# A two-layer decoder step on one Trainium2 core: two small results go through DRAM instead of TensorE, and the sample's low parts take 128 columns

## The chip, the cores and the metric

The kernel runs on one core of one Trainium2 chip. A core has five engines with their own instruction queues: TensorE (PE, matrix products; PEld is its loading of the stationary operand), VectorE (DVE), ScalarE (ACT), GpSimd (POOL) and SyncE (SP, which here issues nearly all DMA transfers). Each engine works through its own queue in the order in which it was written and meets the others through semaphores only. The metric is the device time of one execution in microseconds (us). Smaller is better.

## The reference

One inference step of a decoder trunk with two layers, model width 1024, for 256 prompt tokens and 64 sample tokens (8 sequences of 8) with shared weights. All arrays are float32. Layer 0 mixes tokens with a spatial-gating MLP, layer 1 with a matrix memory (mLSTM); after each comes a gated MLP with a short convolution; each sub-layer has an RMSNorm ahead of it.

```python
def rmsnorm(x, g):
    y = x32 * lax.rsqrt(jnp.mean(x32 * x32, axis=-1, keepdims=True) + EPS)
    return y * g
def chunk_spatial_gating(x, w_in, ln_g, ln_b, w_s, b_s, w_out):       # layer 0
    h = jax.nn.gelu(x @ w_in);  u, v = jnp.split(h, 2, axis=-1)
    v = (v32 - mu) * lax.rsqrt(var + EPS) * ln_g + ln_b               # mean, variance over a row of v
    ws = jnp.where(mask, w_s[:, :L, :L], 0.0)                         # lower triangle, 8 groups of 128 x 128
    mixed = jnp.einsum('gts,bnsgd->bntgd', ws, vc) + b_s
    return (u * mixed) @ w_out, v
def mlstm_mixer(x, ...):                                              # layer 1
    p = x @ w_in            # q, k (then a convolution of width 4), v, an output gate, two small gates
    ...                     # chunkwise matrix memory, norm over heads
    return (o * hn) @ w_out, ...
def trunk(x, ...):
    for i in range(2):
        x = x + mixer_i(rmsnorm(x, norm_mix_g[i]))
        x = x + conv_ffn(rmsnorm(x, norm_ffn_g[i]), ...)
    return rmsnorm(x, final_norm_g), ...
```

Because the mixing over tokens is linear, the kernel applies `ln_b` behind it: the mixed bias is `ln_b` times the sum of a row of the masked mixing matrix `ws`. These row sums (8 groups x 128 rows) are one of the two small results that the change moves.

## The kernel before

**Precision.** Every large product is made from two halves. A float32 value is split into a high part, rounded to the type float32r in which TensorE is fed, and a low part, the rest: `wh` and `wl` for weights (`prefetch`: ScalarE writes `wh`, L180, VectorE subtracts for `wl`, L181), `xh` and `xl` for activations. A product is then `wh*xh + wh*xl + wl*xh`, three matmuls.

**Weights.** They come from DRAM in blocks of 128 x 1024 (`raw`, four buffers, issued on SP's queue), and are split into `wh` and `wl` (three buffers) up to two blocks ahead of the matmuls that use them. A `raw` buffer is free for the next transfer when `wl` has been written.

**Two forms of product.** Most stages hold the weights stationary and stream 320 tokens (`rows`, tile `pm`). For the values of both mixers the tokens are stationary and 512 weight columns stream (tiles `pv` for two groups of 128 prompt tokens and `pvs` for the sample). There are only 64 sample tokens, so the sample's stationary operand `xs` holds 128 columns, its high parts and its low parts. One matmul with `wh` then gives both `xh*wh` and `xl*wh` in different rows of the result, and the rows are added afterwards. A second matmul adds `xh*wl`.

- Layer 0 (`columns`, `first_rows`): `xs` is 64 high columns and then 64 low ones; the matmul with `wl` takes the 64 high columns alone, `pv[2][:64]`. There are four passes `q` over 512 columns of v, each of eight steps `k`; a step is two times three matmuls for the prompt and two for the sample. The final product (`own`, t = 2) does the same with 256 streamed columns.
- Layer 1 (`values`): high and low columns alternate in groups of 16. `xs` has 256 columns per step: 128 with high and low parts for `wh`, 128 with high parts and zeros for `wl`.

**Norms.** The weights of a norm are folded into `xh` and `xl`; the factor per token is applied to a product's result. `norm_cols` (L258) gives the factors as columns `rc` (one per token, tokens on partitions): a sum of squares by three small matmuls against ones (`pc`), VectorE (`ms`) and a power on GpSimd. `norm_row` (L284) makes from them the row `rb`, the factors of all 320 tokens on every partition: it splits `rc`, puts the halves on diagonals (`dg`) and multiplies by ones on TensorE (`pb`). Layer 0 calls `norm_cols` in pass q = 1 and `norm_row` behind pass q = 2; `rb` is first read when block 0 of u is done (L540). Layer 1 has `norm_twice` (L271) as well, which makes one more column of factors `rc2` for the sample in the doubled layout of `xs`.

**Row sums.** `load_ws` fetches the mixing matrix behind pass q = 1 and GpSimd masks it. `row_sums`, behind pass q = 2, splits it (in a pair of the weights' buffers) and multiplies it by ones, four matmuls into `pr`; ScalarE copies the sums, the same on every partition, to `rsum` (`rs_a`, L407). VectorE uses them for `b2` (L522, named `b` in the trace), the bias of a block of mixed values. The first two `b2` stand in VectorE's queue between the splits of weight blocks.

**Order.** TensorE's instructions are pinned to the order in which the program writes them. The queues of the other engines are put in order ahead of time by a scheduler with its own estimate of durations, so a changed dependence can also move other rows. Once built, each queue is fixed: an instruction that waits holds up all that stand behind it.

Of the kernel before, what the change touches and what calls it, by code (L numbers as in the profile page):

```python
# [39 lines left out]
class Net:  # L40
# [215 lines left out]
    def norm_cols(self, parts=None):  # L256

        nc = self.nc  # L258
        parts = parts or [self.acc]
# [11 lines left out]
    def norm_twice(self):  # L271

        nc = self.nc
        acc2 = self.tp.tile([P, P], F32, tag="acc2", name="acc2", bufs=1)
        nc.scalar.copy(self.spread(acc2), self.twice(self.acc[:, TP:]))
        pc = self.psa.tile([P, 512], F32, tag="pa", name="pc2")
        self.mm(pc[:, 0:2], acc2, self.ones[:, :2], True, True)
        ms = self.tp.tile([P, 1], F32, tag="ms2", name="ms2", bufs=1)
        rc = self.tp.tile([P, 1], F32, tag="rc2", name="rc2", bufs=1)
        nc.vector.tensor_scalar(ms, pc[:, 0:1], 1.0 / D, EPS, op0=MULT, op1=ADD)  # L280
        nc.gpsimd.tensor_tensor(rc, ms, self.mhalf, op=ALU.pow)
        self.rc2 = rc

    def norm_row(self):  # L284
# [6 lines left out]
        for half in range(2):  # L291
# [3 lines left out]
            nc.vector.tensor_scalar(dg[:, half, TP:], self.ident[:, 64:], rc[:, half, 2:3], None, op0=MULT)  # L295
# [52 lines left out]
    def residual_norm(self, m, ps, gcol):  # L348
# [3 lines left out]
        if gcol == V_MIX + 8:  # L352
            rows = self.xs[:, m, :].rearrange("p (j g d s) -> p j d g s", j=2, g=4, d=2)
            xh, xl = [x[:, m, TP:].rearrange("p (g s) -> p g s", g=4) for x in (self.xh, self.xl)]
            self.nc.gpsimd.tensor_copy(rows[:, :, 0], xh.unsqueeze(1).to_broadcast([P, 2, 4, 16]))
            self.nc.gpsimd.tensor_copy(rows[:, 0, 1], xl)
# [14 lines left out]
    def layer_a(self):  # L371
        nc, tc, I, O = self.nc, self.tc, self.I, self.O
        with tc.tile_pool(name="ya", bufs=1) as yp, tc.tile_pool(name="la", bufs=1) as lp:
# [8 lines left out]
            rsum = lp.tile([P, NH, P], F32, name="rs_a")  # L382
            trit = lp.tile([P, P], F32, name="trit")
            bdt = lp.tile([P, 64], F32, name="bdt")

            def load_ws():
                nc.sync.dma_start(ws, I["a_ws"])
                nc.sync.dma_start(trit, I["trit"])
# [23 lines left out]
            def first_rows(k, pv, wh, wl):  # L412
# [3 lines left out]
                for i in range(2):  # L416
# [8 lines left out]
                    self.mm(pv[2][:64, c], xs[:, :64], wl[:, c], False, False)  # L425

            def columns(q, k, pv, wh, wl):
# [28 lines left out]
            for q in range(4):  # L456
# [22 lines left out]
                if q == 2:  # L479
                    self.norm_row()  # L480
                    row_sums()
# [151 lines left out]
    def final(self, block, yh, yl, lp):  # L633
# [59 lines left out]
        def own(k, t):  # L693
# [14 lines left out]
            else:  # L708
                xs = yh[:, k, TP:TP + P]
                self.mm(a[:64], xs[:, :64], wl, False, False)  # L710
                self.mm(a, xs, wh, False, last)
# [37 lines left out]
    def layer_b(self):  # L749
# [5 lines left out]
        with ExitStack() as ctx:  # L755
# [8 lines left out]
            mxb = lp.tile([P, 64], F32, name="mxb")  # L764
            gm = lp.tile([P, 4, NH], F32, name="gm")
# [722 lines left out]
```

## Time and profile before

| | before |
|---|---|
| device time, median of 3 runs (lowest to highest) | 942.83 us (942.75 to 943.12) |
| span of the profiled execution, first to last instruction | 941.1 us |
| what lies around the span, taken against the median | 1.7 us |
| TensorE busy | 934.1 us (99%) |
| VectorE, ScalarE, GpSimd busy | 684.5, 508.4, 105.0 us |
| mean granted TensorE clock | 0.998 of full speed |
| DMA moved | 156.46 MB, mean 166 GB/s |

The profile gives no separate time for the profiled execution beside its span; the 1.7 us is the median less the span. Times of day in the trace (such as 49.96) are microseconds from the start of the span. Three things help in reading it. A matmul's recorded duration contains the time its results need to drain, and the next one starts before that is over: what a matmul costs in a row of them is the distance from its start to the next start. `pvs<-wl,xh 128*64 128x512` is a matmul that writes `pvs` from the streamed `wl` (512 columns) with a stationary `xh` of 128 partitions by 64 columns. And the summary of waits names, for an engine and a line, what it waited for, in all, how often, and the longest.

### The profile page before, as it was taken

How to read it: one execution, taken by the hardware profiler on the slowest of the kernel's cores; microseconds unless marked ns; L12 is line 12 of the kernel's file. 1: busy time of each engine (PE TensorE's matmuls, PEld its weight loads, DVE VectorE, ACT ScalarE, POOL GpSimd, SP SyncE). 2: the span in 40 equal slices, each digit the busy share in tenths (PEclk: the TensorE clock that was granted, in tenths of full speed). 3: DMA queues.
4: the chain of work that ended last, by engine and by line, in shares of the span. 5: the costliest groups of instructions: out<-in, count | busy, mean ns of one | idle time of the engine just before them, and what ended most of it. 6: DMA issues, size and time to landing. Idle time of an engine off the chain costs nothing.

```text
span 941.1 us, 16815 instructions
## 1 busy us (share of the span) xinstructions
PE 934.1 (99%) x6361; PEld 902.4 (96%) x6361; DVE 684.5 (73%) x1258; ACT 508.4 (54%) x893; POOL 105.0 (11%) x316
## 2 busy tenths in 40 slices
PE   9999999999999999999999999999999999999997
PEld 8789999999999999998989989989999999999997
DVE  6668975587777765458998988787689777775541
ACT  7567544445544543346777776475656545544332
POOL 3200000011000001113221201000002111100001
PEclk9999999999999999999999999999999999999999
DMA  8746444544555554457675747645474555545621
GB/s 289 223 131 178 133 131 148 155 143 150 156 151 144 154 152 144 146 169 221 210 244 170 232 165 230 228 134 168 151 214 154 144 151 155 146 144 153 202 82 56
DMA packets 58272, 156.46 MB, mean 166 GB/s; under 512 B 6912, under 2 KB 19976, under 8 KB 58192
## 3 DMA queue, kind: packets, MB, share of 16 engines
q1 hardware_dynamic: 58048, 155.13, 53.7%
q8 instruction: 50, 0.82, 0.4%
q10 hardware_dynamic: 144, 0.26, 0.1%
q14 instruction: 30, 0.25, 0.1%
HBM read 143.42 MB, written 11.95 MB: 165 GB/s over the span
## 4 chain that ended last, share of the span: by engine, by line
PE 97%; DVE 1%; POOL 0%; issue 0%; ACT 0%; POOLq 0%; DVEq 0%; ACTq 0%
PE pm L49 76%; PE pv L49 9%; PE pvs L49 3%; PE num L49 2%; PE pyt L49 1%; PE pmix L49 1%; PE py L49 1%; PE pCp L49 1%; PE pcs L49 1%; PE psc L49 0%; PE pw L49 0%; PE phn L52 0%; DVE bcv L903 0%; DVE wl L181 0%; PE pk L52 0%
## 5 line engine op out<-in xcount | busy, mean ns | idle before, releaser
L180 ACT CAST wh<-raw 128x1024 fp32r<-128x1024 f32 (+4 forms) x252 | 255.0, 1013 | 289.4 <-PE pm L49 159.8
L181 DVE TENSOR_TENSOR wl<-raw,wh 128x1024 fp32r<-128x1024 f32 (+4 forms) x252 | 297.0, 1180 | 118.2 <-ACT wh L180 117.2
L49 PE MATMUL pm<-xh,wh 128*128 128x320 f32 x1088 | 338.5, 311 | 0.0
L49 PE MATMUL pm<-xh,wl 128*128 128x320 f32 x1088 | 336.2, 309 | 0.0
L49 PE MATMUL pm<-xl,wh 128*128 128x320 f32 x1088 | 336.1, 309 | 0.0
L49 PEld LDWEIGHTS pm<-xh,wh 128*128 128x128 f32 x1088 | 204.3, 188 | 1.7 <-ACT wh L180 0.5
L49 PEld LDWEIGHTS pm<-xl,wh 128*128 128x128 f32 x1088 | 204.4, 188 | 0.2
L49 PEld LDWEIGHTS pm<-xh,wl 128*128 128x128 f32 x1088 | 204.2, 188 | 0.0
L49 PE MATMUL pm<-yh_f,wh 128*128 128x320 f32 x308 | 95.2, 309 | 0.0
L49 PE MATMUL pm<-yl_f,wh 128*128 128x320 f32 x308 | 94.9, 308 | 0.0
L49 PE MATMUL pm<-yh_f,wl 128*128 128x320 f32 x308 | 94.9, 308 | 0.0
L49 PEld LDWEIGHTS pm<-yl_f,wh 128*128 128x128 f32 x308 | 57.8, 188 | 0.0
L49 PEld LDWEIGHTS pm<-yh_f,wh 128*128 128x128 f32 x308 | 57.8, 188 | 0.0
L49 PEld LDWEIGHTS pm<-yh_f,wl 128*128 128x128 f32 x308 | 57.8, 188 | 0.0
L590 DVE SCALAR_TENSOR_TENSOR fcv<-fpad,vecs,fcv 128x336 f32<-128x336 f32 x88 | 49.7, 565 | 1.5
L49 PE MATMUL pv<-wh,xh 128*128 128x512 f32 (+1 forms) x132 | 50.6, 389 | 0.0
L49 PE MATMUL pv<-wh,xl 128*128 128x512 f32 (+1 forms) x132 | 50.3, 386 | 0.0
L49 PE MATMUL pv<-wl,xh 128*128 128x512 f32 (+1 forms) x132 | 50.1, 385 | 0.0
L346 DVE TENSOR_TENSOR xT<-pm,xT 128x320 f32<-128x320 f32 x38 | 18.6, 491 | 32.9 <-PE pm L49 32.9
L49 PE MATMUL pm<-yhb,wh 128*128 128x320 f32 x128 | 39.9, 312 | 0.0
L49 PE MATMUL pm<-yh_a,wh 128*128 128x320 f32 x128 | 39.6, 309 | 0.0
L49 PE MATMUL pm<-yl_a,wh 128*128 128x320 f32 x128 | 39.5, 309 | 0.0
(340 smaller groups left out, 1461.8 us busy)
## 6 DMA issues: line engine op xcount, KB each, us to landing
raw<-in_f_up SPq DMA_DIRECT2D x88, 512.0 KB, 3.6
raw<-in_b_win SPq DMA_DIRECT2D x32, 512.0 KB, 3.9
raw<-in_f_dn SPq DMA_DIRECT2D x28, 448.0 KB, 3.3
C<-in_C SPq DMA_DIRECT2D x32, 258.0 KB, 5.6
raw<-in_a_win SPq DMA_DIRECT2D x16, 512.0 KB, 3.6
raw<-in_a_wo SPq DMA_DIRECT2D x16, 512.0 KB, 3.7
raw<-in_b_wv SPq DMA_DIRECT2D x16, 512.0 KB, 3.4
out_Cs<-C SPq DMA_DIRECT2D x32, 256.0 KB, 4.6
```

Source lines behind the costliest of these rows:

```text
L49: self.pin(self.nc.tensor.matmul(out, lhsT, rhs, start=start, stop=stop))
L180: self.last_split = nc.scalar.copy(wh[:, c, :], raw[:, c, :])
L181: self.last_low = nc.vector.tensor_tensor(wl[:, c, :], raw[:, c, :], wh[:, c, :].bitcast(F32), op=SUB)
L346: self.nc.vector.tensor_tensor(x, ps[:, :T], x, op=ADD)
L590: nc.vector.scalar_tensor_tensor(cv, pd[:, i:i + NC], self.vec(w + i * KF), cv, op0=MULT, op1=ADD)
```

## The change

1. **Layer 0, norm row** (`norm_sent`): no `norm_row`. SP writes the factors `rc`, 256 prompt and 64 sample values, to a row of 320 numbers in DRAM by two transfers and reads this row back to all 128 partitions as `rb`.
2. **Layer 0, row sums**: the mixing matrix is loaded a second time in its natural layout (`wn`, 512 KB, rows on partitions). GpSimd masks it (`affine_select`), VectorE adds over a row (`tensor_reduce` into `rs8`, 128 x 8), SP writes these 1024 numbers to DRAM, transposed, and reads all of them back to every partition as `rsum`. No split of the matrix and no `pr`.
3. **Layer 1, norm**: the sample's sums of squares are doubled into the layout of `xs` first (`twofold`, a ScalarE copy that was there before inside `norm_twice`), and `norm_cols` takes them for its third column. `rc` then holds the doubled sample factors, `norm_twice` is gone, and `norm_row` takes every sample token once with a loaded 0/1 matrix `pick`.
4. **Sample's low parts**: the matmul with `wl` takes the same 128 columns as the one with `wh`, in layer 0, in layer 1 and in the final product. The term `xl*wl`, left out before, is now added. In layer 1 `xs` shrinks to 128 columns a step, without the zeros that GpSimd wrote at the start of the kernel and with less to copy. In layer 0 and the final product the matmul with `wh` now always comes first.

The core of the diff:

```diff
-    def norm_cols(self, parts=None):
+    def norm_cols(self, side=None):
...
         for t in range(3):
-            for i, a in enumerate(parts):
-                self.mm(pv[:, t, :], self.tokens(a, t), self.ones[:, :2], i == 0, i == len(parts) - 1)
+            a = side if side is not None and t == 2 else self.tokens(self.acc, t)
+            self.mm(pv[:, t, :], a, self.ones[:, :2], True, True)
...
-    def norm_twice(self):
+    def twofold(self):
         acc2 = self.tp.tile([P, P], F32, tag="acc2", name="acc2", bufs=1)
-        nc.scalar.copy(self.spread(acc2), self.twice(self.acc[:, TP:]))
-        pc = self.psa.tile([P, 512], F32, tag="pa", name="pc2")
-        self.mm(pc[:, 0:2], acc2, self.ones[:, :2], True, True)
...
+        self.nc.scalar.copy(self.spread(acc2), self.twice(self.acc[:, TP:]))
+        return acc2
+
+    def norm_sent(self):
+        nc, rows = self.nc, self.I["norm"]
+        nc.sync.dma_start(rows[:, :TP].rearrange("o (t p) -> p (o t)", p=P), self.rc[:, :2])
+        nc.sync.dma_start(rows[:, TP:].rearrange("o p -> p o"), self.rc[64:, 2:])
+        self.rb = self.tp.tile([P, T], F32, tag="rb", name="rb", bufs=1)
+        nc.sync.dma_start(self.rb, rows.to_broadcast([P, T]))
...
             def load_ws():
                 nc.sync.dma_start(ws, I["a_ws"])
+                nc.sync.dma_start(wn, I["a_wsn"])
...
             def row_sums():
-                wh = self.wsp.tile([P, 8, P], F32R, tag="wh", name="wh")
-                wl = self.wsp.tile([P, 8, P], F32R, tag="wl", name="wl")
-                self.split(wh, wl, ws)
-                one = self.ones.bitcast(F32R)
-                for i in range(2):
-                    pr = self.psa.tile([P, 512], F32, tag="pa", name="pr")
-                    for j, w in enumerate((wh, wl)):
-                        self.mm(pr, one, w[:, 4 * i:4 * i + 4, :], j == 0, j == 1)
-                    nc.scalar.copy(rsum[:, 4 * i:4 * i + 4, :].rearrange("p g t -> p (g t)"), pr)
+                nc.gpsimd.affine_select(wn, wn, pattern=[[0, NH], [-1, P]], compare_op=ALU.is_ge, fill=0.0, base=0, channel_multiplier=1)
+                nc.vector.tensor_reduce(rs8, wn, axis=mybir.AxisListType.X, op=ADD)
+                nc.sync.dma_start(I["rsum"].rearrange("g t -> t g"), rs8)
+                nc.sync.dma_start(rsum, I["rsum"].rearrange("g t -> (g t)").unsqueeze(0).to_broadcast([P, NH * P]).rearrange("p (g t) -> p g t", g=NH))
...
             def columns(q, k, pv, wh, wl):
-                if k == 0:
-                    self.mm(pv[2], xs, wh, True, False)
-                self.mm(pv[2][:64], xs[:, :64], wl, False, False)
-                if k > 0:
-                    self.mm(pv[2], xs, wh, False, k == KD - 1)
+                self.mm(pv[2], xs, wh, k == 0, False)
+                self.mm(pv[2], xs, wl, False, k == KD - 1)
...
                 if q == 2:
-                    self.norm_row()
+                    self.norm_sent()
                     row_sums()
...
-                self.norm_cols()
+                self.norm_cols(acc2)
...
                 self.norm_row()
-                self.norm_twice()
...
-                    mm(pv[2], self.xs[:, k, :P], wh[:, i, :], k == 0, False)
-                    mm(pv[2], self.xs[:, k, P:], wl[:, i, :], False, k == KD - 1)
+                    mm(pv[2], self.xs[:, k, :], wh[:, i, :], k == 0, False)
+                    mm(pv[2], self.xs[:, k, :], wl[:, i, :], False, k == KD - 1)
```

Three places in the queues matter below. First, VectorE in layer 0 around the first two `b2`. Before (`wl<-raw` is the low half of a weight block, `st_a<-v_a` the statistics of v):

```order
L181 TENSOR_TENSOR wl<-raw,wh 128x1024 x2
L360 TENSOR_TENSOR wl<-ws_a,wh 128x1024
L451 BN_STATS st_a<-v_a 128x6 x2
L181 TENSOR_TENSOR wl<-raw,wh 128x1024
L522 SCALAR_TENSOR_TENSOR b_855<-rs_a,vecs,bs_a 128x128
L522 SCALAR_TENSOR_TENSOR b_902<-rs_a,vecs,bs_a 128x128
L448 TENSOR_TENSOR vs<-vs,pvs 64x512
```

and in the changed kernel:

```order
L403 TENSOR_REDUCE rs_a<-wn_a 128x8
L446 BN_STATS st_a<-v_a 128x6 x2
L443 TENSOR_TENSOR vs<-vs,pvs 64x512
L181 TENSOR_TENSOR wl<-raw,wh 128x1024
L448 BN_STATS st_a<-v_a 64x6
L181 TENSOR_TENSOR wl<-raw,wh 128x1024 x2
L517 SCALAR_TENSOR_TENSOR b_840<-rs_a,vecs,bs_a 128x128
L517 SCALAR_TENSOR_TENSOR b_887<-rs_a,vecs,bs_a 128x128
L181 TENSOR_TENSOR wl<-raw,wh 128x1024
L446 BN_STATS st_a<-v_a 128x6 x2
```

The two `b2`, which now read what a DMA brings, stand ahead of the low half of the next weight block; before, they stood behind it.

Second, SP's queue from the last small loads of layer 0 on. Before, only loads stand there:

```order
L393 DMA wg<-in_b_wg 128x256
L161 DMA raw<-in_a_wv 128x1024 x2
L507 DMA gB<-in_a_ln_g 64x512
L508 DMA bB<-in_a_ln_b 64x512
L507 DMA gB<-in_a_ln_g 64x512
L508 DMA bB<-in_a_ln_b 64x512
L161 DMA raw<-in_a_wv 128x1024 x2
L161 DMA raw<-in_a_win 128x1024 x8
```

and in the changed kernel (`norm` and `rsum` on the left are writes to DRAM, on the right reads of them):

```order
L396 DMA wg<-in_b_wg 128x256
L161 DMA raw<-in_a_wv 128x1024 x2
L279 DMA norm<-rc 128x2x1
L280 DMA norm<-rc 64x1
L161 DMA raw<-in_a_wv 128x1024
L404 DMA rsum<-rs_a 128x8x1
L282 DMA rb<-norm 128x320
L502 DMA gB<-in_a_ln_g 64x512
L161 DMA raw<-in_a_wv 128x1024
L405 DMA rs_a<-rsum 128x1024
L161 DMA raw<-in_a_win 128x1024
```

The write of the row sums stands behind the third of these weight blocks, and the read of them behind the fourth, ahead of the next one.

Third, TensorE in layer 1 around the norm row, before:

```order
L49 MATMUL pm<-xh,wl 128x320
L49 MATMUL pb<-dg,ones 128x320 x2
L49 MATMUL pc_4665<-ones,acc_4663 128x2
L49 MATMUL pm<-xh,wh 128x320
L49 MATMUL pm<-xl,wh 128x320
```

and in the changed kernel:

```order
L49 MATMUL pm<-xh,wl 128x320
L49 MATMUL pb<-dg,ones 128x320 x2
L49 MATMUL pm<-xh,wh 128x320
L49 MATMUL pm<-xl,wh 128x320
L49 MATMUL pm<-xh,wl 128x320
```

The matmul on the doubled column is gone from behind `pb`; it is now the third one of `norm_cols`, 24 rows earlier, in place of the one on the plain sample columns.

More of the change, by code (lines that the diff above doesn't have):

```diff
@@ L294, in norm_row @@
                 rc[:, half, :2].unsqueeze(2).to_broadcast([P, 2, P]), op=MULT)
-            nc.vector.tensor_scalar(dg[:, half, TP:], self.ident[:, 64:], rc[:, half, 2:3], None, op0=MULT)
+            nc.vector.tensor_scalar(dg[:, half, TP:], self.pick, rc[:, half, 2:3], None, op0=MULT)
         pb = self.psa.tile([P, 512], F32, tag="pa", name="pb")
@@ L382, in layer_a @@
             rsum = lp.tile([P, NH, P], F32, name="rs_a")
+            wn = lp.tile([P, NH, P], F32, name="wn_a")
+            rs8 = lp.tile([P, NH], F32, name="rs8_a")
             trit = lp.tile([P, P], F32, name="trit")
@@ L709, in own @@
                 xs = yh[:, k, TP:TP + P]
[L710 to L711 removed]
+                self.mm(a, xs, wh, False, False)
+                self.mm(a, xs, wl, False, last)
         def leave(t):
@@ L764, in layer_b @@
             mxb = lp.tile([P, 64], F32, name="mxb")
+            self.pick = lp.tile([P, 64], F32, name="pick")
             gm = lp.tile([P, 4, NH], F32, name="gm")
@@ L789, in gates @@
                 RS2 = rp.tile([P, P], F32, name="RS2")
+                acc2 = self.twofold()
+                nc.sync.dma_start(self.pick, I["pick"])
                 nc.sync.dma_start(bif, I["b_if"])
@@ L1352, in run @@
             self.xl = xp.tile([P, KD, T], F32R, name="xl")
-            self.xs = xp.tile([P, KD, 2 * P], F32R, name="xs")
-            nc.gpsimd.memset(self.xs.bitcast(F32), 0.0)
+            self.xs = xp.tile([P, KD, P], F32R, name="xs")
             self.vecs = cp.tile([P, NVEC], F32, name="vecs")
@@ L1458, in _lay_out @@
         [low, (1 - odd) * sign, odd * sign, (1 - odd) * low, odd * low, sign], axis=1)], axis=1).astype(f)
+    a["pick"] = ((tok[:, None] == q[None, :]) & (low[:, None] == 0)).astype(f)
     a["mxb"] = np.where((tok[:, None] // NS == q[None, :] // NS) & (tok[:, None] <= q[None, :]), f(-1e30), f(1e4))
@@ L1471 @@
     O = {k: nc.dram_tensor("out_" + k, s, F32, kind="ExternalOutput").ap() for k, s in _OUTS.items()}
-    I["rows"] = nc.dram_tensor("rows", (8, 456), F32, kind="Internal").ap()
+    for k, v in dict(rows=(8, 456), norm=(1, T), rsum=(NH, P)).items():
+        I[k] = nc.dram_tensor(k, v, F32, kind="Internal").ap()
     with tile.TileContext(nc) as tc:
```

18 lines of the change are left out of this document (6 added, 12 removed).

## The prediction

> **What bounds the kernel now.** I read the page first: the span, the busy shares, the chain that ended last; then the summary of TensorE's waits.
>
> ```profile
> span 941.1 us, 16815 instructions
> PE 934.1 (99%) x6361; PEld 902.4 (96%) x6361; DVE 684.5 (73%) x1258; ACT 508.4 (54%) x893; POOL 105.0 (11%) x316
> PE 97%; DVE 1%; POOL 0%; issue 0%; ACT 0%; POOLq 0%; DVEq 0%; ACTq 0%
> PE pw L49 <- PEq L1469: 0.8, 1, 0.8
> ```
>
> TensorE is busy from 0.8 us on and waits for nothing until its last matmul; its only wait is the start-up one. So whatever leaves its queue leaves the time, from start to next start, and work that moves among the other engines counts only where it makes TensorE wait. There are two questions: how many start-to-start microseconds go, and whether the new trips through DRAM are late for somebody that TensorE needs.
>
> A measurement of this kernel tells about 0.2% from no change: 1.9 us of 942.83.
>
> **Term 1, the norm row and the row sums of layer 0 leave TensorE.** The timeline between pass q = 2 and q = 3:
>
> ```profile
> 49.72 0.40 PE L49 MATMUL pvs<-wh,xh 128*128 128x512 f32 x1
> 49.96 0.46 PE L49 MATMUL pb<-dg,ones 128*128 128x320 f32 x2
> 50.25 0.39 PE L49 MATMUL pr<-wh,ones 128*128 128x512 f32 x1
> 51.18 0.40 PE L49 MATMUL pv<-wh,xh 128*128 128x512 f32 x1
> ```
>
> Two `pb` and four `pr` matmuls occupy 51.18 - 49.96 = 1.22 us. The durations (0.40) overlap, so adding those would give nearly double. Afterwards `pv` starts where `pb` did. (The two `pb` take 0.29 us of it, 0.15 us for each matmul of 320 columns.) Gain: **1.22 us**. The copies, splits and diagonals that go on VectorE and ScalarE count nothing by themselves, since TensorE hides them.
>
> **Term 2, 128 instead of 64 columns for the sample's low parts.** Layer 1 already uses 128 columns in both matmuls of its sample, so the two forms can be compared at an equal eight matmuls of 512 columns per step. The tile's groups, by window and over the run, and the starts of the first `pv` of a step:
>
> ```profile
> L49 PE MATMUL pvs<-wl,xh x24: 397/398/398, 21.5 to 65.4; 128*64 128x512 f32 x24
> L49 PE MATMUL pvs<-wl,xs x32: 389/389/393, 433.1 to 621.5; 128*128 128x512 f32 x32
> 29.78 0.40 PE L49 MATMUL pv<-wh,xh 128*128 128x512 f32 x1
> 48.12 0.40 PE L49 MATMUL pv<-wh,xh 128*128 128x512 f32 x1
> 433.36 0.39 PE L49 MATMUL pv<-wh,xh 128*128 128x512 f32 x1
> 440.61 0.39 PE L49 MATMUL pv<-wh,xh 128*128 128x512 f32 x1
> L49 PE MATMUL pvs<-wl,xh 128*64 128x512 f32 x30 | 11.9, 397 | 0.0
> ```
>
> Layer 0: ten steps in 48.12 - 29.78 = 18.34 us, 1.834 a step. Layer 1: four steps in 440.61 - 433.36 = 7.25 us, 1.8125 a step. Layer 0 is 0.0215 us a step slower, and the narrow matmul is itself the long one (398 against 389 ns). With 128 columns I expect layer 1's pace: 30 steps at 512 columns (the count of the last row) x 0.0215 = **0.65 us** gained. The bounds are 0 (the pace has another cause in that stage) and 0.65; I take the upper one, because the extra time sits on the narrow matmul. At 256 columns no difference shows, so the final product counts 0:
>
> ```profile
> L49 PE MATMUL pyt<-wl,yh_f 128*64 128x256 f32 x12 | 2.8, 278 | 0.0
> L49 PE MATMUL pyt<-wh,yh_f 128*128 128x256 f32 x24 | 6.2, 280 | 0.0
> L49 PEld LDWEIGHTS pvs<-wl,xh x34: 134/134/223, 5.6 to 65.2; 128*64 128x64 f32 x34
> L49 PEld LDWEIGHTS pvs<-wh,xh x34: 188/188/330, 5.4 to 65.4; 128*128 128x128 f32 x34
> ```
>
> The last two rows speak against the change: loading 128 stationary columns takes 188 ns, 64 take 134. If the 54 ns were exposed, 34 matmuls here and 22 in the final product would cost 56 x 0.054 = 3.0 us. But TensorE starts a matmul every 0.229 us here while it loads, and layer 1 pays nothing for its 188 ns, so I price the load at 0; its cover is the 0.229 us matmul before it.
>
> The Trainium skill (TensorE: Matmul & The Clock Gate, section on LDWEIGHTS) says that a weight load's time grows with its columns and not with its rows; the two load rows agree (134 and 188 ns). By that rule, with the load exposed, the sum would turn from a gain into a loss of about 1 us; that is a rival below.
>
> The Trainium skill (TensorEngine Tiling (Array Packing), Key Properties) says that a change of tiling mode drains TensorE. If a 64-column matmul counts as another mode, two drains of 0.40 - 0.23 = 0.17 us a step would be worth about 10 us over 30 steps. The trace has only 0.0215 us a step, so term 2 cannot give more than 0.65.
>
> **Term 3, layer 1's second norm column.**
>
> ```profile
> 425.08 0.30 ACT L275 COPY acc<-acc 128x128 f32<-128x128 f32 x1 [0.91 <-DVE acc L241]
> 425.50 0.72 PE L49 MATMUL pc<-ones,acc 128*128 128x2 f32 x6
> 429.98 0.28 PE L49 MATMUL pc<-ones,acc 128*128 128x2 f32 x2
> 430.35 0.31 PE L49 MATMUL pm<-xl,wh 128*128 128x320 f32 x1
> ```
>
> Gone is the `pc` at 429.98 (one matmul, two records). The second matmul behind it starts at 430.35; without it the first would start at 429.98 and the second 0.15 later (term 1). Gain 0.37 - 0.15 = 0.22 us. New: the third `pc` of the first group reads ScalarE's copy. It ended at 425.38, and the third pair of records starts about two thirds through the 0.72 us from 425.50, near 425.9. The cover is half a microsecond; without it TensorE would wait for as much as the copy comes late. I take **0.2 us**, bounds -0.3 and 0.22. `pick`, loaded beside layer 1's other constants, and the smaller copies and missing memset on GpSimd touch no wait of TensorE: 0.
>
> **The hand-off, the term that can eat the gain.** The factors' row is harmless: `rb` is first read at
>
> ```profile
> 70.28 0.49 DVE L540 TENSOR_TENSOR ur<-pm,rb 128x320 f32<-128x320 f32 x1
> ```
>
> and its read stands in SP's queue near 40 us; with the longest landing below it is there some 20 us early. The row sums are not. Their write stands behind the third of the `raw` loads, their read waits for that write, and the two `b2` that need the read stand on VectorE directly ahead of the low half of a weight block. Where they wait, that `wl` waits, then TensorE. The rows that time this:
>
> ```profile
> 26.61 0.42 SPq L388 DMA_DIRECT2D trit<-in_trit  x1
> DMA to landing us min/median/max: 4.1/4.5/5.0
> 28.27 0.87 POOL L268 TENSOR_TENSOR rc<-ms,mhalf 128x3 f32<-128x3 f32 x1 [12.89 <-DVE ms L267]
> 39.46 2.40 SPq L161 DMA_DIRECT2D raw<-in_a_wv  x2
> 447.30 0.26 SPq L863 DMA_DIRECT2D rows<-RS  x1
> 449.47 5.12 SPq L1059 DMA_DIRECT2D mb<-rows  x3
> DMA to landing us min/median/max: 3.2/5.5/6.7
> bs_a<-in_a_bs SPq DMA_DIRECT2D x1, 512.0 KB, 5.3
> n<-in_n SPq DMA_DIRECT2D x1, 32.0 KB, 2.9
> bif<-in_b_if SPq DMA_DIRECT2D x1, 1.1 KB, 2.4
> q1 hardware_dynamic: 58048, 155.13, 53.7%
> 43.94 1.23 DVE L181 TENSOR_TENSOR wl<-raw,wh 128x1024 fp32r<-128x1024 f32 x1 [2.44 <-ACT wh L180]
> 46.52 1.05 ACT L359 CAST wh<-ws_a 128x1024 fp32r<-128x1024 f32 x1 [2.62 <-PE pvs L49]
> 54.87 0.40 PE L49 MATMUL pv<-wh,xh 128*128 128x512 f32 x1
> 52.48 0.61 DVE L522 SCALAR_TENSOR_TENSOR b<-rs_a,vecs,bs_a 128x128 f32<-128x128 f32 x2
> L1009 POOL TENSOR_SCALAR_AFFINE_SELECT w<-w 128x128 f32<-128x128 f32 x16 | 6.4, 419 | 37.7 <-ACT w L1006 27.2 <-DVE kz L1049 10.5
> ```
>
> Issue: the third `raw` goes at 39.46 (its buffer is freed by VectorE), so the write goes near 39.5. The row sums exist by then: GpSimd is free at 29.1 (behind `rc`), the second matrix is issued where `trit` was and has landed by 31.6 (5.0 us is the longest of the `raw` loads in that stretch, the first of the two landing rows; the second one is `mb`'s), the mask costs eight times 0.42 = 3.4 us at most, VectorE's sum 1.23 like a `wl` of as many values: 36.2.
>
> Write: this kernel has one hand-off of that kind already, `rows`, issued at 447.30, its reader released at 449.47: 2.2 us, the lower bound. But `rs8` goes out as 1024 pieces of 4 bytes, 64 for each of 16 DMA engines. The mean packet took 0.537 x 16 x 941.1 us / 58048 = 139 ns for 2.7 KB: 64 x 0.139 = 8.9 us more, the upper bound. From 1.1 to 32 KB (2 to 8 packets per engine) landing grows by 0.5 us, 83 ns a packet. A piece of 4 bytes should lie below that; I take 45 ns: 2.9 us. Landed at 39.5 + 2.2 + 2.9 = 44.6 (41.7 to 50.6).
>
> Read: `bs_a` is the same transfer, 512 KB broadcast: 5.3 us; the broadcasts of `rows` took 3.2 to 6.7. So `rs_a` is there at **49.9** (44.9 to 57.3).
>
> Need: VectorE reaches the `b2` at 45.2, behind the `wl` of 43.94. The next block's high half will be cast at 46.5, where the row sums' matrix was cast before. Its low half is needed by the third matmul of its unit, which started at 54.87 before and moves up by 1.22 and some 0.5: 53.15 + 0.46 = 53.6. Less 1.23 for `wl` and 0.61 for both `b2`, `rs_a` may come as late as **51.8**. So VectorE idles some 4 us and TensorE does not notice: 0, with 1.9 us to spare. At the upper end the wait is 57.3 - 51.8 = 5.5 us.
>
> **Sum.** 1.22 + 0.65 + 0.2 + 0 = 2.07 us off the span of 941.1: 939.0. The median of the runs stands 1.7 above that span, so **940.8 us**.
>
> **The rivals.**
>
> *Late, but little.* `rs_a` lands between 51.8 and 55.8; TensorE waits up to 4 us before the second unit of pass q = 3. At 83 ns a piece it lands at 52.3, so this needs no extreme. For it: four-byte pieces, the weights in the same queue. Against: the `rows` hand-off had a weight block ahead of it too and took 2.2. Time 941 to 944.7, mostly 941.8.
>
> *Late by much, slower.* The same wait from a landing later than 53.9 costs more than all gains, and later than 55.8 it shows (over 0.2%). Upper bounds of write and read together: 940.8 + 5.5 = 946.3. Against it: it needs the mean packet's price for four bytes and the slowest broadcast.
>
> *The narrow matmul isn't the cause.* Layer 0's slower step stays; 1.42 us gained, 941.4: no measurable change.
>
> *The wider load is exposed.* 3.0 us lost, 1.4 gained: 944.4. Layer 1's pace speaks against it.
>
> *The doubled column is late.* TensorE waits for ScalarE's copy in layer 1: 941.3. That the change does not do what it says is excluded for the matmuls: they are gone from TensorE's queue.
>
> **How the numbers follow.** Forecast 0.52, own range 940.5 to 941.2. Late by little 0.25, late by much 0.07, cause elsewhere 0.11, load exposed 0.02, column late 0.03. The threshold of 940.94 lies inside the forecast's own range, 0.14 above its centre: I give 0.45 of the 0.52 to faster and, for small waits, 0.02 of the first rival. Faster 0.47, within 0.2% 0.46, slower 0.07. The range reaches over most of "late by little": 940.3 to 943.0.
>
> **What would show it.** Right: no `pr` row and only two `pb<-dg` records; steps of layer 0 at 1.81 us and the `wl` matmul of `pvs` at 389 ns; no new row in TensorE's waits; VectorE idle ahead of `b2` for DMA `rs_a`, ending before 51.8. Wrong: TensorE waiting for `wl` near 53 us, with `rs_a` landing after 52; steps still at 1.83; a wait of `pc` for `acc` near 424; or stalls at a place that none of these terms names.

## The result: 10.3 us slower

| | before | after |
|---|---|---|
| device time, median (lowest to highest) | 942.83 us (942.75 to 943.12) | 953.16 us (952.66 to 954.13) |
| ratio, with its 95% interval | | 1.011 (1.0098 to 1.0123) |
| span of the profiled execution | 941.1 us | 951.6 us |

The forecast was 940.8 us with a range up to 943.0. The time lies 10 us above that range, in the direction of the rival that had a chance of 0.07, and above that rival's own upper bound of 946.3.

The first lines of the page after, its chain of waits by engine, and the row of the summary of TensorE's waits that is new:

```profile
span 951.6 us, 16797 instructions
PE 934.6 (98%) x6353; PEld 904.4 (95%) x6353; DVE 681.2 (72%) x1252; ACT 505.8 (53%) x888; POOL 105.7 (11%) x315
PE 92%; DMA 3%; DVE 2%; POOL 1%; issue 1%; ACT 0%; SPq 0%; POOLq 0%; DVEq 0%; ACTq 0%
PE pv L49 <- DVE wl L181: 10.1, 1, 10.1
```

TensorE waits once, for 10.1 us, for the low half of a weight block. Who was late shows on the way back. First VectorE's and TensorE's timelines (start, duration, what; in brackets the idle time before it and what ended that):

```profile
43.30 1.23 DVE L181 TENSOR_TENSOR wl<-raw,wh 128x1024 fp32r<-128x1024 f32 x1 [1.93 <-ACT wh L180]
62.01 0.61 DVE L517 SCALAR_TENSOR_TENSOR b<-rs_a,vecs,bs_a 128x128 f32<-128x128 f32 x2 [17.48 <-DMA rs_a<-rsum]
62.54 1.22 DVE L181 TENSOR_TENSOR wl<-raw,wh 128x1024 fp32r<-128x1024 f32 x1
```

```profile
53.31 0.39 PE L49 MATMUL pv<-wh,xl 128*128 128x512 f32 x1
63.81 0.79 PE L49 MATMUL pv<-wl,xh 128*128 128x512 f32 x1 [10.11 <-DVE wl L181]
```

VectorE stood 17.5 us at the first two `b2` until the row sums were back. The `wl` that TensorE wanted at 53.5 (one start behind 53.31) stands right behind them. Then SyncE's timeline, its wait, and the landings of the transfers (KB each, us from issue to landing):

```profile
34.49 0.47 SPq L280 DMA_DIRECT2D norm<-rc  x1
39.42 0.35 SPq L161 DMA_DIRECT2D raw<-in_a_wv  x1
39.81 0.43 SPq L404 DMA_DIRECT2D rsum<-rs_a  x1
55.70 0.32 SPq L405 DMA_DIRECT2D rs_a<-rsum  x1
```

```profile
SPq L405 <- DMA rsum<-rs_a: 10.3, 1, 10.3
norm<-rc SPq DMA_DIRECT2D x1, 0.2 KB, 9.3
rsum<-rs_a SPq DMA_DIRECT2D x1, 4.0 KB, 15.8
rs_a<-rsum SPq DMA_DIRECT2D x1, 512.0 KB, 6.2
```

The row sums' write, 4 KB, was issued at 39.81 as forecast (39.5), but took 15.8 us to land (forecast 5.1, upper bound 11.1). The read took 6.2 (forecast 5.3). So `rs_a` was there at 61.9 instead of 49.9. The norm factors' write is slow in the same way: 9.3 us for a quarter of a KB.

The wait is not the whole loss. The windows of TensorE's clock around it (length, busy time and count of PE, PEld, DVE, ACT, POOL; then the granted clock, the DMAs' share, GB/s):

```profile
53.70:57.11 3.41, 0.00 (x0) 0.00 (x0) 0.00 (x0) 0.00 (x0) 0.00 (x0) 1.00 0.48 107
57.11:60.52 3.41, 0.00 (x0) 0.00 (x0) 0.00 (x0) 0.00 (x0) 0.00 (x0) 0.50 0.99 270
60.52:63.94 3.42, 0.13 (x1) 0.13 (x1) 1.94 (x4) 0.00 (x0) 0.00 (x0) 0.50 0.71 127
63.94:67.35 3.41, 3.41 (x8) 2.68 (x9) 3.32 (x5) 1.61 (x2) 0.00 (x0) 0.50 0.56 165
67.35:70.76 3.41, 3.41 (x16) 2.80 (x15) 2.44 (x3) 1.20 (x2) 0.00 (x0) 1.00 0.69 190
```

After 3.4 idle microseconds the granted clock fell to one half, and it stayed there until 67.35, 3.5 us into the work. In the window from 63.94 eight matmuls ran instead of the sixteen of the next one. The nine starts from 63.81 to 67.37 take 3.56 us; at the pace ahead of the wait (sixteen starts from 49.45 to 53.08, 0.227 us each) they would take 1.81. That is 1.75 us more.

The starts that the account below rests on, the first of them before the change and the others after it:

```profile
65.87 0.31 PE L49 MATMUL pm<-xh,wh 128*128 128x320 f32 x1
67.37 0.39 PE L49 MATMUL pv<-wl,xh 128*128 128x512 f32 x1
76.03 0.30 PE L49 MATMUL pm<-xh,wh 128*128 128x320 f32 x1
```

**The account**, from starts on TensorE: the first `pm` of layer 0 moved from 65.87 to 76.03, by +10.16. Up to the start of pass q = 3 the change had gained 1.73 (51.18 became 49.45), and another 0.17 by its faster steps after that. The interval from 53.31 to 63.81 is 10.50 instead of 0.23, 10.27 more, and the half clock adds 1.75. The sum is -1.73 - 0.17 + 10.27 + 1.75 = +10.12. From there to behind layer 1's norm 0.17 is gained, 0.2 is lost in small steps up to 920 us, and the final product loses 0.33, which makes +10.5, the difference of the spans.

### The profile page after: what moved, and what is told of

Its sections match the earlier page's. It is cut to its first block, busy times and chain, and to the rows that moved or that the text cites. A ratio compares the mean times of both kernels' runs of the same rounds, so it can differ in the third digit from the quotient of the medians.

```text
span 951.6 us, 16797 instructions
## 1 busy us (share of the span) xinstructions
PE 934.6 (98%) x6353; PEld 904.4 (95%) x6353; DVE 681.2 (72%) x1252; ACT 505.8 (53%) x888; POOL 105.7 (11%) x315
## 4 chain that ended last, share of the span: by engine, by line
PE 92%; DMA 3%; DVE 2%; POOL 1%; issue 1%; ACT 0%; SPq 0%; POOLq 0%; DVEq 0%; ACTq 0%
PE pm L49 75%; PE pv L49 7%; PE pvs L49 2%; PE num L49 2%; DMA rsum<-rs_a 2%; PE pyt L49 1%; PE pmix L49 1%; PE py L49 1%; DVE wl L181 1%; DMA wn_a<-in_a_wsn 1%; DMA gB<-in_a_ln_g 1%; PE pCp L49 1%; PE pcs L49 0%; PE psc L49 0%; PE pw L49 0%
## 5 line engine op out<-in xcount | busy, mean ns | idle before, releaser
L49 PE MATMUL pv<-wl,xh 128*128 128x512 f32 (+1 forms) x132 | 50.7, 390 | 10.1 <-DVE wl L181 10.1
L49 PEld LDWEIGHTS pv<-wl,xh 128*128 128x128 f32 x132 | 25.1, 193 | 15.5 <-DVE wl L181 10.5
```

The lines of the kernel that those rows point to most:

```text
L49: self.pin(self.nc.tensor.matmul(out, lhsT, rhs, start=start, stop=stop))
```

## The experiments

Theory A: all of the loss is VectorE standing at `b2`, and what makes the row sums late is how the small results are written to DRAM. A1: pieces of 4 bytes that lie next to each other in DRAM wait for each other and hold up the DMA queues behind them, so that the norm factors' 320 pieces delay the row sums' 1024. A2: the row sums' own write takes 15.8 us. Rivals: B, another part of the change costs the time; C, SyncE's wait for the write does harm by itself, since weight loads stand behind it.

### Is it the wait at `b2`?

**`hold`.**

```diff
+                with self.behind(self.ur):
                     nc.vector.scalar_tensor_tensor(b2, rsum[:, g:g + 1, :], ...)
...
-                nc.vector.tensor_tensor(t, ps[:, :T], self.rb, op=MULT)
+                self.ur = nc.vector.tensor_tensor(t, ps[:, :T], self.rb, op=MULT)
```

> The change, with each `b2` held on VectorE behind the `ur` of its pass through the block loop, so that the low halves of layer 0's last pass no longer stand behind it; nothing else is altered. Theory A (the whole loss is VectorE standing at the first `b2` until the row sums are back): TensorE's wait of 10.1 us goes, and with it the slow matmuls behind it (1.9 us): 953.16 - 10.1 - 1.9 = 941.1 us, although the write of the row sums lands as late as before. Theory B (another part of the change costs the time: the norm factors' trip, the wider low parts): a time above 950. Theory C (SyncE's wait for the write, which keeps the weight loads behind it back until 55.7 us, hurts by itself): TensorE waits for a `wh` or `wl` near 58 to 66 us, 942 to 947.

Measured: 946.42 us (945.84 to 948.38); ratio to before 1.0038 (1.0023 to 1.0053). Most of the loss is gone with nothing but VectorE's order changed, so B falls. But A's 941.1 isn't reached, as C said. TensorE's waits and SyncE's timeline of this run:

```profile
PE pm L49 <- ACT wh L180: 2.3, 1, 2.3
PE pm L49 <- DVE wl L181: 1.1, 2, 0.7
```

```profile
57.21 0.32 SPq L405 DMA_DIRECT2D rs_a<-rsum  x1
57.59 0.42 SPq L161 DMA_DIRECT2D raw<-in_a_win  x1
```

The write landed 17.4 us after its issue, and a weight load stood behind the read until 57.59. Its block came late for the first products of the next stage. So the write costs twice: at VectorE, and, once that is healed, at SyncE.

**`tsums`.** The row sums as in the kernel before (`wh`, `wl`, split, four `pr`, two copies in place of mask, sum, write and read).

```diff
-                nc.gpsimd.affine_select(wn, wn, ...)
-                nc.vector.tensor_reduce(rs8, wn, ...)
-                nc.sync.dma_start(I["rsum"].rearrange("g t -> t g"), rs8)
-                nc.sync.dma_start(rsum, I["rsum"]...to_broadcast([P, NH * P])...)
+                self.split(wh, wl, ws)
+                for i in range(2):
+                    for j, w in enumerate((wh, wl)):
+                        self.mm(pr, one, w[:, 4 * i:4 * i + 4, :], j == 0, j == 1)
+                    nc.scalar.copy(rsum[:, 4 * i:4 * i + 4, :]..., pr)
```

> The change with the row sums back on TensorE (four `pr`, two copies and the split, as in the kernel before); the norm factors' trip, the wider low parts and the doubled column stay. Theory A: no wait of TensorE; the four `pr` cost 0.94 us again: 953.16 - 10.1 - 1.9 + 0.9 = 942.1 us. Theory B: above 950.

Measured: 942.41 us (942.01 to 942.68); ratio 0.9992 (0.9982 to 1.0001); no wait of TensorE but its start. As A said. The norm factors' trip by itself, with a landing of 9.2 us, hurts nobody.

### What makes the write late?

**`trow`.**

```diff
-                    self.norm_sent()
+                    self.norm_row(self.ident[:, 64:])
```

> The change with the norm factors' row of layer 0 back on TensorE (two `pb`, the split and the diagonals, as in the kernel before); the row sums still go through DRAM in 1024 pieces of 4 bytes. Theory A1 (the pieces of the norm factors, 320 of 4 bytes, hold up the transfers behind them, so that the pieces of the row sums start only near 45 us): without them the row sums' write starts near 40.5 and lands near 50.5 instead of 55.6, the wait falls from 10.1 to about 5, the slow stretch behind it stays between 1 and 1.9 us: 947.5 to 948.5 us. Theory A2 (the row sums' own pieces take 15.8 us, whatever is ahead): landing still 15.8 us, 953.4 us.

Measured: 948.21 us (946.93 to 948.94); ratio 1.0051 (1.0036 to 1.0066).

```profile
PE pv L49 <- DVE wl L181: 3.8, 1, 3.8
rsum<-rs_a SPq DMA_DIRECT2D x1, 4.0 KB, 11.0
```

The same 1024 pieces land in 11.0 instead of 15.8 us, at 49.85. The time falls by 4.95 although two `pb` are back. A2 falls as it stands: of the 15.8 us some 5 are the norm factors' pieces ahead, and 11.0 are the row sums' own. By the records of single DMA packets the row sums' pieces start near 46 in the kernel after and in 39 to 41 here. The pieces themselves are quick, 7 to 9 ns each in these records; it is what follows that stands still.

**`joined`.** Each partition's eight sums lie side by side in DRAM.

```diff
-    rsum=(NH, P)
+    rsum=(P, NH)
-                nc.sync.dma_start(I["rsum"].rearrange("g t -> t g"), rs8)
+                nc.sync.dma_start(I["rsum"], rs8)
-    ... rsum[:, g:g + 1, :] ...
+    ... rsum[:, :, g:g + 1].rearrange("p t g -> p g t") ...
```

> The change with the row sums kept in DRAM by token and then group, so that each partition writes one piece of 32 bytes (128 pieces instead of 1024); the broadcast read is the same 512 KB, and `b2` reads every eighth value of its row. The order of the instructions on VectorE is that of the change. Theory A1 (small pieces are the price, and those of the norm factors stay ahead): the write can start near 45 us and lands near 46.5, `rs_a` near 52.5; TensorE waits 0 to 1 us: 941.1 to 942.2 us. Theory A3 (the landing comes from the queue or the bytes, not from the pieces): 15.8 us again and 953 us.

Measured: 946.69 us (943.0 to 948.85); ratio 1.0037 (1.0023 to 1.0051). The landings, of an execution that took 946.93:

```profile
norm<-rc SPq DMA_DIRECT2D x1, 0.2 KB, 9.7
rsum<-rs_a SPq DMA_DIRECT2D x1, 4.0 KB, 8.3
rs_a<-rsum SPq DMA_DIRECT2D x1, 512.0 KB, 7.3
```

The direction is right, so A3 falls, but I was 3 us too early: the write landed at 48.2 instead of 46.5, since the norm factors' pieces were done only at 44.3, and the read took 7.3 instead of 5 to 6, beside the transfers that had queued up. `rs_a` came at 55.5, and TensorE waited 3.8 us, as long as in `trow`.

**`half`, `apart`, `grain`, `apart64`.** Four ways to lay out small pieces, all with the norm factors' row on TensorE, so none of its small pieces stand ahead. The edits of the write, without those of the fill and the read:

```diff
 # half: four of the eight groups
+                nc.sync.dma_start(I["rsum"].rearrange("g t -> t g")[:, :4], rs8[:, :4])
 # apart: rsum=(NH * P, P), each sum at the start of a row of 512 bytes
+                nc.sync.dma_start(I["rsum"].rearrange("(g t) c -> t g c", g=NH)[:, :, 0:1], ...)
 # grain: rsum=(2 * NH, P), a partition's sums in every second word of its own 64 bytes
+                nc.sync.dma_start(I["rsum"].rearrange("a (t g c) -> (a t) g c", g=NH, c=2)[:, :, 0:1], ...)
 # apart64: rsum=(P, P), each sum at the start of 64 bytes
+                nc.sync.dma_start(I["rsum"].rearrange("a (b c) -> (a b) c", c=16).rearrange("(g t) c -> t g c", g=NH)[:, :, 0:1], ...)
```

> Built on the run with the norm factors' row back on TensorE, whose write of 1024 pieces landed 11.0 us after its issue. Here only four of the eight groups' row sums are written (512 pieces of 4 bytes); the read broadcasts these four groups twice, so the bias of groups 4 to 7 is left with wrong sums. Theory N (each small piece costs its share of the time): landing near 2.4 + 8.6 / 2 = 6.7 us. Theory L (the pieces of one group, 128 neighbouring values from 128 partitions, wait for each other, and the groups run side by side): landing stays near 11 us; the norm factors' 320 pieces, 9.2 us, already speak for it.

> Built on the same run as the half. All 1024 pieces of 4 bytes are written, but each into a row of its own in DRAM, 512 bytes from the next; the rows are filled once, early, by a copy of other data, and the read takes 4096 bytes of that, so the row sums that `b2` uses are left out. Theory N: landing 11.0 us again. Theory L (neighbours in memory wait for each other): landing 3 to 5 us, the transfers behind it start at once, `rs_a` is there near 49 and TensorE waits for nothing.

> As the run before it, but the eight sums of a partition go to every second word of 64 bytes that belong to this partition alone: 1024 pieces of 4 bytes, neighbours by eights from the same partition. Theory N: 11.0 us. Theory L as a matter of the 128 partitions meeting in one line: 3 to 5 us. Theory L as a matter of any two pieces meeting in 64 bytes: between, with eight instead of 16 pieces in 64 bytes some 6 us.

> Norm factors' row on TensorE, and 1024 pieces of 4 bytes, each in 64 bytes of its own; eight of them, from eight partitions, share 512 bytes. The 64 KB are filled once, early, by a copy of other data, and the read takes its first 4096 bytes, so the row sums that `b2` uses are left out. So far: 128 pieces in 512 bytes took 11.0 us from issue to landing, 64 (from eight partitions) 6.9, and with each in 512 bytes of its own the landing came 0.7 us after the last piece had started. If pieces wait for each other within 64 bytes: 3 to 4 us. If within 512 bytes: 8 in 512 bytes, about 1 us of waiting more than that, 4 to 5 us. If it is the number of pieces after all: 11 us.

| run | pieces of 4 bytes | in the same 64 bytes | issue to landing |
|---|---|---|---|
| `trow` | 1024 | 16, from 16 partitions | 11.0 us |
| `half` | 512 | 16, from 16 partitions | 10.0 us |
| `grain` | 1024 | 8, from one partition | 6.9 us |
| `apart64` | 1024 | 1 | 5.0 us, a weight block ahead of it |
| `apart` | 1024 | 1 (in 512 bytes) | 5.4 us, a weight block ahead of it |

Each of these four new kernels was executed once. The first three landings are rows of the profile. For the last two the trace's signals of landing were read: sixteen for each transfer, the last at 45.00 in `apart64` (issued at 39.98) and at 49.57 in `apart` (issued at 44.14). Half as many pieces save 1.0 of 11.0 us, so the number isn't the price (6.7 was expected of it). By the records of single packets the last piece had started at 40.4 in `trow`, 38.4 in `half`, 40.8 in `grain`, 43.3 in `apart64` and 48.7 in `apart`. From there to the landing it took 9.4, 8.5, 5.0, 1.7 and 0.8 us.

What happens in between shows in the DMA engines' busy share, 40 slices of 38 to 52 us, in tenths: `trow` (with what they moved in the line below), then `grain`, then `apart64`.

```profile
DMA  4000067036900090000000048493444043290568
GB/s 176 23 0 0 0 6 6 0 41 164 117 0 23 29 176 12 0 0 0 0 0 0 0 82 94 23 47 12 23 12 35 12 23 35 12 94 12 105 234 351
```

```profile
DMA  3698405700000000000009059555599999879999
```

```profile
DMA  0000000904899999655996468997493399999997
```

In `trow` the pieces go out by 41. A weight load issued at 42.04 gets a short stretch near 43, and after that nothing moves up to 45.7. From there to 50 the engines are busy by the digits, but move 12 to 94 GB/s: single packets of the weight load that take microseconds. In `grain` nothing moves from 41 to 45.3. In `apart64`, with as many pieces, the engines work on from 41 without a stop. So N falls, and L holds as far as this: the same 1024 pieces of 4 bytes land late when they lie close together in DRAM and soon when they lie apart, and while the close ones are late, what stands behind them in the queue hardly moves. TensorE tells of it as well: 1.1 us of waiting for a `wl` in `half`, 1.2 in `grain`, none in `apart64`.

How wide the stretch is within which pieces must not meet isn't settled. In `trow` and `grain` the crowd in 512 bytes goes with that in 64 (128 and 16 pieces, 64 and 8). `apart64`, with 8 and 1, should tell the two apart, and it lies between: its first piece started 2.3 us after issue instead of 0.9 in `trow`, since a weight block was ahead; without these 1.4 its 5.0 us would be 3.6, as expected of 64 bytes. But its landing came 0.9 us later behind the last piece than that of `apart`, and about 1 us was expected of 512. The layouts also spread the pieces over 4, 8, 64 and 512 KB in all, and no run separates this from the distance to the next piece.

The Trainium skill (DMA: Bandwidth & Descriptors, Specifications) says that a transfer below 512 bytes is done by reading, changing and writing back. That could make neighbours wait for each other. But pieces below 512 bytes don't stall as such: those of `apart` had landed 0.8 us after the last had started. That the late landings come from this mechanism is argued and not shown.

In `apart` the early copy of 512 KB also moved the row sums' own steps and a weight block later. TensorE waited 1.7 us for a `wh` and 0.5 for a `wl`, so its 944.9 us says nothing about the write.

### A version that beats both

**`joined_hold`** has the two edits of `joined` and `hold` together.

> Pieces of 32 bytes for the row sums and `b2` held on VectorE, together; the norm factors' trip stays in front. The two runs that did one of these alone each left a wait: 3.8 us (`rs_a` at 55.5, the norm factors' pieces ahead of it) and 2.3 and 1.1 us (SyncE's wait until 57.2 kept a weight load back). Theory A: with the write landed at 48.3 SyncE goes on in time and nobody waits for `b2`: TensorE waits for nothing, 942.83 less the 2.1 us of the three gains and plus 0.3 for the final product = 941.1 us. Theory D (the norm factors' stall alone already makes a weight block late): a wait of `wl` or `wh` between 53 and 66 us, 942 to 945.

Measured: 941.31 us (941.0 to 942.52); ratio 0.9981 (0.9971 to 0.999). As A said; D falls. The write landed at 48.8, so SyncE's next weight load went at 49.2 and nobody was late (TensorE's only wait beside its start, 0.3 us for a `wh`, lies in the first 20 us).

**`norm12`** takes the cause away instead: both results in larger pieces, `b2` where the change has it.

```diff
-        nc.sync.dma_start(rows[:, :TP].rearrange("o (t p) -> p (o t)", p=P), self.rc[:, :2])
-        nc.sync.dma_start(rows[:, TP:].rearrange("o p -> p o"), self.rc[64:, 2:])
+        nc.sync.dma_start(sent, self.rc)                       # 128 x 3 in DRAM
+        nc.sync.dma_start(rb3, sent.rearrange("p t -> (p t)").unsqueeze(0).to_broadcast([P, 3 * P]))
+        nc.gpsimd.tensor_copy(self.rb[:, :TP]..., by[:, :2, :])    # by: rb3, token group first
+        nc.gpsimd.tensor_copy(self.rb[:, TP:], by[:, 2, 64:])
```

> Both trips in larger pieces and nothing held: the row sums as 128 pieces of 32 bytes, the norm factors as 128 pieces of 12 bytes (all three values of a partition side by side, the broadcast read of 192 KB put in the row's order by two GpSimd copies). `b2` stands where the change has it. Theory L (pieces that share a stretch of DRAM wait for each other: 16 in 64 bytes took 9 us, 8 took 5, 2 took about 1): with 5 to 6 pieces in 64 bytes the norm factors hold the queues 2 to 4 us instead of 6 to 7, the row sums land near 45, `rs_a` near 51; TensorE waits 0 to 0.5 us: 941.1 to 941.6 us. Theory D (the wait of 3.8 us that was left with 32-byte row sums is not the norm factors' doing): 946 again.

Measured: 941.51 us (940.95 to 941.92); ratio 0.9984 (0.9975 to 0.9993). The landings, and the first `b2` on VectorE:

```profile
norm<-rc SPq DMA_DIRECT2D x1, 1.5 KB, 3.8
rsum<-rs_a SPq DMA_DIRECT2D x1, 4.0 KB, 3.2
```

```profile
45.00 0.83 DVE L520 SCALAR_TENSOR_TENSOR b<-rs_a,vecs,bs_a 128x128 f32<-128x128 f32 x2 [0.65 <-DMA rs_a<-rsum]
```

TensorE waits for nothing. The write landed at 37.8, far earlier than the 45 I had expected. Two things make the difference: SyncE's queue now issues the row sums' write right behind the norm factors', ahead of the next weight load, and the norm factors' 12-byte pieces, five to six in 64 bytes, show no stall instead of one of 2 to 4 us: they landed 0.8 us after the last of them had started, as soon as the lone pieces of `apart`. So the number of pieces in 64 bytes does not set the stall by itself. Whether the size of the pieces, their number (128 instead of 1024) or the engine that writes them matters as well stays open.

### The wider low parts in the final product

**`narrow_end`** (on `joined_hold`) and **`both_joined`** (on `norm12`, with `hold`) put the sample's low parts back on 64 columns in the final product alone:

```diff
-                self.mm(a, xs, wh, False, False)
-                self.mm(a, xs, wl, False, last)
+                self.mm(a[:64], xs[:, :64], wl, False, False)
+                self.mm(a, xs, wh, False, last)
```

> Pieces of 32 bytes and `b2` held, which ran at 941.3 us, and in the final product the sample's low parts on 64 columns in front again, as in the kernel before. If the 128 columns are why the final product's 110 matmuls took 13.37 us in every kernel with the change and 13.04 before: 13.04 again and 941.0 us. If the pace there has another reason (the smaller `xs`, which moves what stands behind it in SBUF): 13.37 stays and 941.3 us.

> All of it: row sums in pieces of 32 bytes, norm factors in pieces of 12, `b2` held, the final product's low parts on 64 columns. TensorE waits for nothing but its start. 942.83 - 1.22 - 0.65 - 0.2 = 940.8 us if the narrow final product is back at 13.04 us, 941.1 if not; theory D: above 942 by a wait for a weight block near 55 to 66 us.

Measured: 941.38 us (940.88 to 942.06), ratio 0.9983 (0.9974 to 0.9992), and 941.52 us (941.24 to 942.26), ratio 0.9986 (0.9977 to 0.9995). None of the four fast kernels can be told from another by its time. From the first to the last start the final product takes 13.04 us before, 13.37 in the kernels with 128 columns there, and 13.25 in these two. The first and the last start before, after and in `narrow_end`:

```profile
921.81 1.18 PE L49 MATMUL pyt<-xh,yh_f 128*64 128x256 f32 x8
934.84 0.28 PE L49 MATMUL pyt<-wl,yh_f 128*128 128x256 f32 x1
932.05 1.32 PE L49 MATMUL pyt<-xh,yh_f 128*128 128x256 f32 x9
945.42 0.27 PE L49 MATMUL pyt<-wl,yh_f 128*128 128x256 f32 x1
920.25 1.19 PE L49 MATMUL pyt<-xh,yh_f 128*64 128x256 f32 x8
933.50 0.28 PE L49 MATMUL pyt<-wl,yh_f 128*128 128x256 f32 x1
```

So the columns explain 0.12 of the 0.33 us; the rest, a pace of 0.120 instead of 0.117 us also in matmuls that are the same in both, isn't explained.

## Why the prediction was wrong

**Term 1, 1.22 us: right.** No `pr` is left, `pv` follows `pvs` directly, and the start of pass q = 3 moved up by 1.73, which is 1.22 and the 0.51 of term 2 so far.

**Term 2, 0.65 us: right in layer 0, wrong in the final product.** The tile's groups and two steps of the kernel after:

```profile
L49 PE MATMUL pvs<-wl,xh x34: 283/389/628, 5.8 to 75.8; 128*128 128x512 f32 x30, 128*128 128x256 f32 x4
49.45 0.39 PE L49 MATMUL pv<-wh,xh 128*128 128x512 f32 x1
53.08 0.39 PE L49 MATMUL pv<-wh,xh 128*128 128x512 f32 x1
```

The matmul takes 389 ns, and two steps take 3.63 us, 1.81 each. The weight load of 188 ns stays hidden there. The layer gained 0.51 and 0.17, as forecast. The final product, priced 0, costs 0.33, of which the section before this gives 0.12 to the columns and leaves 0.21 unexplained. Together that is a gain of about 0.35 instead of 0.65.

**Term 3, 0.2 us: right.** In the kernel after:

```profile
435.71 0.72 PE L49 MATMUL pc<-ones,acc 128*128 128x2 f32 x6
439.90 0.46 PE L49 MATMUL pb<-dg,ones 128*128 128x320 f32 x2
440.34 0.31 PE L49 MATMUL pm<-xl,wh 128*128 128x320 f32 x1
```

The first `pc` of layer 1 is late by 10.21 us (425.50 before), the second matmul behind `pb` by 9.99 (430.35 before): 0.22 gained, as the working of the term had it. The third `pc` doesn't wait for ScalarE's copy.

**The hand-off, 0 us: this step failed.** Its frame held. The write was issued at 39.81 (39.5 forecast), the read took 6.2 us (5.3), and TensorE came to the matmul in question at 53.5 (53.6). What was wrong is the price of the write, 2.2 us and 64 x 45 ns, with a bound of 64 x 139 ns. It treats the pieces as things that each occupy a DMA engine for a while. The runs show another quantity: how close together the pieces lie in DRAM. The same 1024 pieces took 11.0 us side by side (`trow`), 6.9 with eight in 64 bytes (`grain`), and 5.0 and 5.4, a weight block ahead, with one in 64 or in 512 bytes. Side by side they all had started by 40.4 and landed 9.4 us later, and the engines took little new meanwhile. Why closeness costs stays open. The `rows` hand-off, the one with 2.2 us, had written eight pieces of 256 bytes (2 KB), and was no model for single values. The own pieces make 11.0 us (`trow`). That this is close to my upper bound for the write, 2.2 + 8.9 = 11.1, is chance: half the pieces should have landed near 6.7 by it, and took 10.0.

**"The factors' row is harmless" failed in the same step.** I looked at when `rb` is read, and not at what its write does to those behind it. It made the row sums' write some 5 us later, 15.8 instead of 11.0, and so took it past every bound that I had set.

**The rivals.** "Late by much, slower" is what happened, by its mechanism and at its place, and its bound of 946.3 came from the same prices: a landing of 11.1 and a wait of 5.5 us. With the norm factors' pieces out of the way (`trow`) there were 11.0 and 3.8 us, and 948.2 us: the bound lacked the half clock behind a long wait, 1.75 us in the kernel after and 1.6 in `trow`. With two `pb` (0.29) and the final product (0.33), 940.8 + 3.8 + 1.6 + 0.6 makes some 946.8; the rest of the 948.2 is not accounted for. The others did not happen: the narrow matmul was the cause in layer 0, the load isn't exposed there, the column wasn't late.

**The question that I did not ask** is how far `b2` could be moved. Its result is used only in the next stage. Had it stood there, and the write in larger pieces, the forecast of 940.8 would have been near: 941.31 in `joined_hold`.

## What to carry to other kernels

When a small result goes through DRAM, look at the piece that one partition writes, and at where its neighbours land: lay it out so that each partition writes one contiguous piece, and put the permutation into the reader's access pattern, where it cost next to nothing here (0.83 instead of 0.61 us for two `b2`). Price such a write with everything that stands behind it in the queue, the next hand-off and the weight loads as well. And an instruction that reads the result belongs in its engine's queue where the result is needed, not where it could first run.

## What the runs showed that I had not expected

- **320 or 1024 values of 4 bytes, neighbours in DRAM from different partitions, landed 9 to 11 us after issue** (15.8 behind another such write), and the DMA engines stood nearly still for several of them. 128 pieces of 32 bytes and 128 of 12 bytes, side by side, landed in 3.2 and 3.8 us (`norm12`). Pieces of 4 bytes that lie 64 or 512 bytes apart landed 1.7 and 0.8 us after the last had started, and the engines worked on.
- **TensorE's granted clock fell to one half in windows of 3.41 us.** It fell after a wait of 10.1 us (three windows at one half), and after waits of 3.8 us in `trow` and `joined` (one each), but not after waits of 2.3 us in `hold` and 1.1 in `half`. In `trow` it fell only at 59.28, when the matmuls had gone on since 58.53:

```profile
55.87:59.28 3.41, 0.75 (x3) 0.66 (x4) 2.55 (x5) 0.00 (x0) 0.00 (x0) 1.00 1.02 251
59.28:62.69 3.41, 3.41 (x9) 2.68 (x9) 3.29 (x5) 1.76 (x2) 0.00 (x0) 0.50 0.67 179
62.70:66.10 3.40, 3.40 (x16) 2.79 (x15) 2.15 (x2) 1.05 (x1) 0.00 (x0) 1.00 0.79 228
```

The Trainium skill (TensorE: Matmul & The Clock Gate, Part 1: The HAM clock gate) says that the clock is halved after an idle window of 3.4 us, and that the windows run freely; these rows agree, except that the window ahead of the half clock in `trow` wasn't wholly idle: TensorE was busy for 0.75 of its 3.41 us.
